# Output projection in three and five blocks, FF1 units between its tiles, an earlier x reload and a chained second product

## The chip, the cores and the metric

The kernel runs on one core of a Trainium2 chip. The metric is device time in microseconds (us); lower is better. Five engines work side by side, each through its own list in order: TensorE (PE, matrix products), VectorE (DVE), ScalarE (ACT), GpSimd (POOL) and SyncE (SP), whose list here is that of nearly all DMA transfers. PE takes its operands from SBUF and writes to banks of PSUM, which DVE or ACT then read.

## The reference

One layer over x of 1024 tokens x 1024 channels in float32:

```
u = rms_norm(x) @ W_in                    # columns split over three mixers
mixed = concat(stick_breaking_attention, retention, conformer_conv)
x = x + mixed @ W_out                     # 1024 x 1024
h = rms_norm(x)
x = x + square(relu(h @ W1)) @ W2         # 1024 x 4096 (FF1), 4096 x 1024 (FF2)
```

## The kernel before

All tensors are held transposed: channels on the 128 partitions, tokens along the free axis. Each float32 operand is split into a high part (cast to fp32r on ACT) and a low part (a subtraction on DVE or POOL), and each product is three matmuls, hi x hi, hi x lo, lo x hi (`mm3`, L107 to L110), mostly of 128x128 by 128x512. `w_split` (L141) splits weights, `x_split` (L703 to L706) splits quarters of x.

**Order of the work.** The program is written as a sequence, and a scheduler that simulates the engines reorders it for each engine (L1087). Buffers are named tiles (`xh0`, `P6`, `DM`, ...) of which one user must be through before the next writes; banks are named g, t, z, o, with two of each.

**Output projection** (L743 to L769). The mixed channels are eight blocks k of 128: attention 0 and 1, retention 2, 3, 6, 7, conv 4 and 5. Two passes of four blocks each. A pass has 16 tiles (8 of output channels, dt, times 2 halves of tokens, hf), each of 12 matmuls into a bank g and an addition to x2 (L758, the eviction). `tick` (L228) puts a tile among steps of attention, conv and retention that are still due. After each dt of the second pass `x2_ready` (L711) stores the tile to DRAM (x2d), squares it (ACT), adds the squares up (POOL, L720), scales it in place (ACT, L721) and forms the sums and differences that FF1 needs (POOL, L726 to L735; x_split). `x2_late` splits the rest.

**FF1.** Seven products of blocks (Strassen's scheme) instead of eight: 16 pairs p of 128-row tiles of W1, for each the products 1, 5, 6, 2, 7, 4, 3, each a unit of 12 matmuls over kk = 0 to 3, which read `x_split` tiles (i, kk). `hidden` makes the relu and its square, `right` forms the seven right operands of FF2 (POOL) and stores them as f{p}_{i} in DRAM.

**FF2.** Units are (chunk of pairs, product i, pair n), each with 12 matmuls into four banks. Five chunks of fifteen pairs go through the seven products in the order 5, 6, 3, 7, 1, 4, 2; products 1, 6 and 7 are gathered in separate accumulator tiles and added to the quadrants of x2 at the end by POOL (L964, L967). The last pair is done by eight plain block products (`run_last`, 96 matmuls). x is loaded back from DRAM when the first unit of FF2 is due (L1047 to L1055), `ahead` loads W2 tiles and f.

A `DMA` row of SP issues when its target is free and its source is ready; the rows behind it wait.

## Time and profile before

| | us |
|---|---|
| time, median of 3 runs | 1193.98 (1193.6 to 1194.81) |
| profiled execution, its own time | 1193.62 |
| its span | 1191.8 |
| PE busy | 1142.1 (96%) |
| DVE busy | 888.1 (75%) |
| POOL busy | 594.9 (50%) |
| ACT busy | 491.9 (41%) |

The span is what the profiler saw between the first and the last instruction; the rest of the execution's time lies around it. The mean granted clock of PE over the span is 0.984 of full speed (2.4 GHz); where the clock shows less, part of that stretch ran at 1.2 GHz. A share of busy time is a mean over stages. The output projection ends near 535, FF1 begins near 518 and ends near 862, FF2 ends at 1188.

### The profile page before, as it was taken

What the parts mean: (1) busy time and instruction counts of PE and PEld (TensorE: products, weight loads), DVE (VectorE), ACT (ScalarE), POOL (GpSimd) and SP (SyncE); (2) the same over time, 40 slices, a digit from 0 to 9 for tenths busy, and PEclk for the clock granted to TensorE, in tenths of its full rate; (3) what the DMA queues carried; (4) which work ended last, traced back from release to release, by engine and by line L of the source; (5) the groups of instructions that cost most, each with busy time, mean ns of one, the idle gap of its engine ahead of it and who ended that gap; (6) DMA issues with size and microseconds to landing.
All of it is one profiled execution on the core that took longest, in us unless ns stands there. A gap on an engine that the chain in (4) does not pass through costs nothing.

```text
span 1191.8 us, 17699 instructions
## 1 busy us (share of the span) xinstructions
PE 1142.1 (96%) x6388; PEld 991.6 (83%) x6388; DVE 888.1 (75%) x1346; ACT 491.9 (41%) x925; POOL 594.9 (50%) x473
## 2 busy tenths in 40 slices
...
GB/s 279 37 37 36 54 40 59 19 70 51 50 54 63 28 196 52 62 89 54 140 152 150 145 147 165 153 166 136 382 233 125 176 115 166 171 120 120 97 18 141
DMA packets 62871, 135.55 MB, mean 114 GB/s; under 512 B 7104, under 2 KB 11840, under 8 KB 62784
## 3 DMA queue, kind: packets, MB, share of 16 engines
...
q14 instruction: 37, 0.30, 0.1%
...
## 4 chain that ended last, share of the span: by engine, by line
PE 78%; DVE 13%; DMA 3%; issue 3%; ACT 2%; POOL 1%; SPq 0%; DVEq 0%; ACTq 0%; POOLq 0%
PE g L108 12%; PE g L110 12%; PE g L109 12%; PE t L108 4%; PE t L109 4%; PE t L110 4%; PE z L109 4%; PE z L110 4%; PE z L108 4%; PE o L109 3%; PE o L110 3%; PE o L108 3%; DVE DM__508_2651 L513 3%; DVE wlo L141 2%; PE o L354 2%
## 5 line engine op out<-in xcount | busy, mean ns | idle before, releaser
L141 POOL TENSOR_TENSOR wlo<-wraw,whi 128x512 fp32r<-128x512 f32 x67 | 100.3, 1510 | 96.4 <-ACT whi L140 96.2
L141 DVE TENSOR_TENSOR wlo<-sum,whi 128x512 fp32r<-128x512 f32 x75 | 77.3, 1032 | 86.9 <-ACT whi L140 86.9
L141 DVE TENSOR_TENSOR wlo<-wr,whi 128x512 fp32r<-128x512 f32 x88 | 86.9, 991 | 20.6 <-ACT whi L140 20.6
L140 ACT CAST whi<-sum 128x512 fp32r<-128x512 f32 x75 | 46.2, 618 | 115.5 <-POOL sum L783 48.1
L140 ACT CAST whi<-wr 128x512 fp32r<-128x512 f32 x88 | 53.3, 620 | 78.8 <-PE g L109 25.6
L324 POOL TENSOR_TENSOR be<-be,kp 128x512 f32<-128x512 f32 (+3 forms) x48 | 46.1, 962 | 78.3 <-DVE kp L320 49.9
L788 POOL TENSOR_TENSOR sum<-wr 128x512 f32<-128x512 f32 x16 | 22.7, 1419 | 98.8 <-DMA wr<-in_w_ff_dram 90.6
L140 ACT CAST whi<-wraw 128x512 fp32r<-128x512 f32 x68 | 41.9, 621 | 65.8 <-PE g L109 27.7
L320 DVE TENSOR_TENSOR_SCAN kp<-kp 128x512 f32<-128x512 f32 (+3 forms) x48 | 51.1, 1067 | 10.6 <-ACT kp L313 10.0
L513 DVE SCALAR_TENSOR_TENSOR DM__508_2651<-glu,vec,DM__508_2651 128x512 f32<-128x512 f32 x60 | 53.3, 926 | 0.1
L783 POOL TENSOR_TENSOR sum<-sum,wr 128x512 f32<-128x512 f32 x21 | 29.6, 1408 | 45.3 <-DVE wlo L141 45.3
L155 POOL TENSOR_TENSOR rs<-ss,nhalf 128x4 f32<-128x4 f32 (+1 forms) x36 | 37.9, 1055 | 25.4 <-DVE ss L621 14.5
L513 DVE SCALAR_TENSOR_TENSOR glu<-glu,vec 128x512 f32<-128x512 f32 x60 | 47.8, 857 | 0.0
L783 POOL TENSOR_TENSOR sum<-wr,sum 128x512 f32<-128x512 f32 x21 | 35.4, 1686 | 11.2 <-DVE wlo L141 11.2
L313 ACT ACTIVATE kp<-z 128x512 f32<-128x512 f32 (+3 forms) x48 | 23.6, 494 | 16.7 <-PE z L310 13.0
L108 PE MATMUL g<-whi,xh__12_100 128*128 128x256 f32 x82 | 25.3, 309 | 2.8 <-DVE P__107_556 L288 0.9
L108 PE MATMUL g<-whi,xh__34_250 128*128 128x256 f32 x82 | 23.3, 285 | 2.5 <-ACT xh__34_250 L174 2.5
L314 ACT ACTIVATE be<-z 128x512 f32<-128x512 f32 (+3 forms) x48 | 23.5, 493 | 4.9 <-PE t L335 4.9
L110 PE MATMUL g<-whi,xl__53_362 128*128 128x256 f32 x82 | 23.3, 286 | 1.6 <-DVE xl__53_362 L175 1.6
L335 PE MATMUL t<-ident,be 128*128 128x128 f32 x144 | 24.2, 274 | 0.1
L110 PE MATMUL g<-whi,xl__46_323 128*128 128x256 f32 x82 | 23.5, 288 | 0.0
L108 PE MATMUL g<-whi,xh__52_361 128*128 128x256 f32 x82 | 23.5, 287 | 0.0
...
## 6 DMA issues: line engine op xcount, KB each, us to landing
...
wraw<-in_w_in_dram SPq DMA_DIRECT2D x52, 256.0 KB, 3.2
...
wraw<-in_w_out_dram SPq DMA_DIRECT2D x16, 256.0 KB, 2.6
...
P__29_215<-in_xT_dram SPq DMA_DIRECT2D x1, 512.0 KB, 3.5
...
```

The source lines that it names most:

```text
L108: TE.matmul(out, lh, rh, start=start, stop=False, skip_group_check=on)
L109: TE.matmul(out, lh, rl, start=False, stop=False, skip_group_check=on)
L110: TE.matmul(out, ll, rh, start=False, stop=stop, skip_group_check=on)
L140: S.copy(hi, raw)
L141: (lo_engine or GP).tensor_tensor(out=lo, in0=raw, in1=hi.bitcast(F32), op=ALU.subtract)
L155: GP.tensor_tensor(out=out, in0=in_, in1=nhalf[:, 0:in_.shape[1]], op=ALU.pow)
L320: V.tensor_tensor_scan(rev, rev, rev, kp[:, n:n + 1], op0=ALU.mult, op1=ALU.bypass)
L324: GP.tensor_tensor(out=be[:, 0:n], in0=be[:, 0:n], in1=kp[:, 1:n + 1], op=ALU.mult)
L335: TE.transpose(pt[:, j * P:j * P + P], be[:, j * P:j * P + P], ident)
L354: TE.matmul(po[:, oc], lw, rhs, start=st["first"], stop=(jg == 0 and j == order[-1] and w is wtl))
L513: V.scalar_tensor_tensor(out=acc, in0=src, scalar=vec[:, o:o + 1], in1=acc, op0=ALU.mult, op1=ALU.add)
L783: (eng or GP).tensor_tensor(out=o, in0=x, in1=y, op=ALU.subtract)
```

## The change

1. The first pass takes blocks 0 to 2 (bank g, 9 matmuls in a tile), the second 3 to 7 (bank o, 15 matmuls). Weights come by quarters of a host-packed 512-column source; their low part is made on POOL in the first pass and on DVE in the second. Blocks are split by halves, 3, 4 and 5 inside the first pass.
2. The first three units of FF1 stand behind tiles dt = 5, 6, 7 of the second pass. The statistics of the second norm follow at unit 5. The `hidden` of product 2 of pair 0 moves to product 7, behind them.
3. In `x2_ready` the addition of squares (7 of 128x1024) and the first subtraction of dt >= 4 (4 of 128x512) go from POOL to DVE; two splits go to `x2_late`.
4. x is loaded back five units before the end of FF1, into other buffers. W2 and f loads follow written points (`transfers`), f with ten buffers instead of nine.
5. FF2 has four chunks (3, 4, 4, 5 pairs), all sixteen pairs by seven products, in the order 1, 5, 6, 3, 7, 2, 4. Products 1, 6, 7, 4 go on in one set of banks, 5 and 3 in the other, 2 after them; each intermediate sum is added to one quadrant of x2. The accumulator tiles, the POOL additions and `run_last` go.

The diff, cut to its core:

```diff
+    def w_quarter(lo_engine=None):
+
+        if not quarters:
+            c = wpos[1]
+            wpos[1] += 1
+            w_dma(c + RAW)
+            hi, lo = w_split(raws[c], lo_engine)
+            quarters.extend((hi[:, P * h:P * h + P], lo[:, P * h:P * h + P]) for h in range(4))
+        return quarters.pop(0)
...
+    def split_mixed(k, halves_=(0, 1)):
+        if k not in mh:
+            mh[k], ml[k] = slot(where[k][0], dt=F32R), slot(where[k][1], dt=F32R)
+        for hf in halves_:
+            cs = slice(512 * hf, 512 * hf + 512)
+            src = conv_part(k - 4, hf) if k in (4, 5) else mixed[k][:, cs]
+            S.copy(mh[k][:, cs], src)
+            V.tensor_tensor(out=ml[k][:, cs], in0=src, in1=mh[k][:, cs].bitcast(F32), op=ALU.subtract)
...
-    for k in range(4):
-        split_mixed(k)
-
-
-
-    XS = {1: ("xh0", "xl0", "xh1", "xl1"), 5: ("xh2", "xl2", "xh3", "xl3"), 6: ("P10", "P11", "P12", "P13"),
-          2: ("P14", "P15", "P16", "P17"), 7: ("P18", "P19", "P4", "P5"), 4: ("P0", "P1", "P2", "P3"),
-          3: ("P6", "P7", "P8", "P9")}
+    split_mixed(0)
+    for hf in range(2):
+        for k in (1, 2):
+            split_mixed(k, (hf,))
...
-            sq2[0] = pg.tile([P, T], F32, tag="glu0", name="sq2")
-            S.activation(sq2[0], x, AF.Square)
+            sq = sq2[0] = pg.tile([P, T], F32, tag="glu0", name="sq2")
         else:
             sq = slot(("DM", "glu1")[dt % 2])
-            S.activation(sq, x, AF.Square)
-            GP.tensor_tensor(out=sq2[0], in0=sq2[0], in1=sq, op=ALU.add)
+        S.activation(sq, x, AF.Square)
...
-            return
-        t, b12 = x2[kk][:, 0:512], x2[kk][:, 512:1024]
-        GP.tensor_tensor(out=t, in0=b, in1=t, op=ALU.subtract)
-        x_split(6, kk, t)
-        x_split(2, kk, a)
-        GP.tensor_tensor(out=b12, in0=b, in1=b12, op=ALU.subtract)
-        x_split(7, kk, b12)
-        GP.tensor_tensor(out=t, in0=a, in1=t, op=ALU.subtract)
+        else:
+            t, b12 = x2[kk][:, 0:512], x2[kk][:, 512:1024]
+            V.tensor_tensor(out=t, in0=b, in1=t, op=ALU.subtract)
+            x_split(6, kk, t)
+            x_split(2, kk, a)
+            GP.tensor_tensor(out=b12, in0=b, in1=b12, op=ALU.subtract)
+            if kk < 2:
+                x_split(7, kk, b12)
+            GP.tensor_tensor(out=t, in0=a, in1=t, op=ALU.subtract)
+        if dt > 0:
+            V.tensor_tensor(out=sq2[0], in0=sq2[0], in1=sq, op=ALU.add)
...
     def x2_late():
+        for kk in range(2, 4):
+            x_split(7, kk, x2[kk][:, 512:1024])
         for kk in range(4):
             x_split(4, kk, x2[kk][:, 0:512])
         for kk in range(4):
             x_split(3, kk, x2[kk + 4][:, 512:1024])
 
...
-    pend = parts(4)
-    for pi in range(2):
-        for dt in range(NK):
-            w = pend[:2]
-            del pend[:2]
-            for hf in range(2):
-                tsl = slice(512 * hf, 512 * hf + 512)
-
-                def run():
-                    ps = bank("g")
-                    for q in range(4):
-                        k = 4 * pi + q
-                        cs = slice((q % 2) * P, (q % 2) * P + P)
-                        wh, wl = w[q // 2]
-                        mm3(ps, wh[:, cs], wl[:, cs], mh[k][:, tsl], ml[k][:, tsl], q == 0, q == 3)
-                    V.tensor_tensor(out=x2[dt][:, tsl], in0=ps, in1=x2[dt][:, tsl], op=ALU.add)
-                    if wpos[1] < len(sources) or halves:
-                        pend.append(w_part())
-                tick(run)
-            if pi == 1:
-                x2_ready(dt)
-        if pi == 0:
-            while steps:
-                tick()
-            for k in range(4, 8):
-                split_mixed(k)
-    x2_late()
...
+
+    def out_weights(pi, dt):
+        ks = range(EARLY) if pi == 0 else range(EARLY, NK)
+        return {k: w_quarter(GP if pi == 0 else V) for k in ks}
+
+    def out_proj(pi, dt, hf):
+        tsl = slice(512 * hf, 512 * hf + 512)
+        w = taken[pi, dt]
+        ps = bank("o" if pi else "g")
+        for k in w:
+            mm3(ps, w[k][0], w[k][1], mh[k][:, tsl], ml[k][:, tsl], k == min(w), k == max(w))
+        V.tensor_tensor(out=x2[dt][:, tsl], in0=ps, in1=x2[dt][:, tsl], op=ALU.add)
+
+    jobs = [(pi, dt) for pi in range(2) for dt in range(NK)]
+    taken[0, 0] = out_weights(0, 0)
+
+    def out_job(pi, dt):
+        n = jobs.index((pi, dt))
+        if n + 1 < len(jobs):
+            taken[jobs[n + 1]] = out_weights(*jobs[n + 1])
+        for hf in range(2):
+            tick(lambda: out_proj(pi, dt, hf))
+        if pi == 1:
+            x2_ready(dt)
+
+    for dt in range(NK):
+        out_job(0, dt)
+        if dt in (1, 5, 6):
+            split_mixed({1: 3, 5: 4, 6: 5}[dt])
+    while steps:
+        tick()
+    for hf in range(2):
+        for k in (6, 7):
+            split_mixed(k, (hf,))
...
-    chunks = [[0, 1], [2, 3, 4], [5, 6, 7, 8], [9, 10, 11], [12, 13, 14]]
-    order2 = (5, 6, 3, 7, 1, 4, 2)
+
+    chunks = [[0, 1, 2], [3, 4, 5, 6], [7, 8, 9, 10], [11, 12, 13, 14, 15]]
+    order2 = (1, 5, 6, 3, 7, 2, 4)
...
-    WS2 = [("wr", 4)] * 4 + [(t, 1) for t in XS[4] + XS[3]]
-    nw2 = [0]
-    nfi = [0]
-    FI = ("DM", "xh4", "xl4", "xh5", "xl5", "xh6", "xl6", "xh7", "xl7")
+    C = XS[1] + XS[5]
+    WS2 = (["wr", "wr"] + list(XS[7] + XS[4] + XS[3]) + ["wr", "wr", "DM", "P4", "P5"])
+    WS2 = ["wr", "wr", "glu0", "DM", "P4", "P5"] + WS2 * 2
+    RS = XS[6][2:4] + XS[2][0:2]
+    FI = FS[0] + XS[2][2:4] + FS[1]
+    nw2, nfi, nrs, nsum = [0], [0], [0], [0]
 
...
     def run_ff2(c, i, n):
-        s = {5: "X", 3: "X", 1: "X", 2: "X", 6: "Y", 7: "Y", 4: "Y"}[i]
-        first = i in (5, 1, 6, 4)
+        s = {1: "X", 6: "X", 7: "X", 4: "X", 5: "Y", 3: "Y", 2: "Y"}[i]
+        first = i in (1, 5, 2)
         if n == 0 and first:
             ps2[s] = [bank(t) for t in {"X": "ggtt", "Y": "zzoo"}[s]]
...
+        rh, ch = {1: (0, 0), 2: (0, 0), 5: (1, 1), 7: (1, 1), 6: (0, 1), 3: (0, 1), 4: (1, 0)}[i]
         for dt in range(4):
-            ps = ps2[s][dt]
-            if i in (1, 6, 7):
-                a = a_part(i, dt)
-                if c == 0:
-                    S.copy(a, ps)
-                else:
-                    add(a, a, ps)
-            else:
-                a = c_part({5: 5, 3: 3, 2: 2, 4: 4}[i], dt)
-                add(a, ps, a)
-        if c == len(chunks) - 1 and i == 1:
-            for dt in range(4):
-                for to, src in ((6, 1), (7, 1)):
-                    GP.tensor_tensor(out=a_part(to, dt), in0=a_part(to, dt), in1=a_part(src, dt), op=ALU.add)
-            for to, src in ((3, 6), (4, 7), (5, 7)):
-                for dt in range(4):
-                    GP.tensor_tensor(out=c_part(to, dt), in0=c_part(to, dt), in1=a_part(src, dt), op=ALU.add)
-
...
-    def run_last(k, dh):
-        for dt in range(4):
-            ps = bank(("z", "o", "g", "t")[dt])
-            cs = slice(dt * P, dt * P + P)
-            for j in range(2):
-                wh, wl = last_w[dh][j]
-                fh, fl = last_f[k][j]
-                mm3(ps, wh[:, cs], wl[:, cs], fh, fl, j == 0, j == 1)
-            a = c_part({(0, 0): 2, (0, 1): 4, (1, 0): 3, (1, 1): 5}[k, dh], dt)
-            add(a, ps, a)
-            r = (4 * dh + dt) * P
-            nc.sync.dma_start(d["yT"][r:r + P, 512 * k:512 * k + 512], a)
+            a = x2[4 * rh + dt][:, 512 * ch:512 * ch + 512]
+            add(a, ps2[s][dt], a)
+            if c == len(chunks) - 1 and i in (3, 7, 2, 4):
+                r = (4 * rh + dt) * P
+                nc.sync.dma_start(d["yT"][r:r + P, 512 * ch:512 * ch + 512], a)
...
+    prep = {"1": prep_ff1, "2": prep_ff2}
+    run = {"1": run_ff1, "2": run_ff2}
+    f_order = [(chunks[c][n], i) for c in range(len(chunks)) for i in order2 for n in range(len(chunks[c]))]
+    nf = [0]
...
+    w2_at = {n1 + 6: 3, n1 + 10: 4, n1 + 14: 5, n1 + 18: 6, n1 + 25: 7, n1 + 29: 8, n1 + 33: 9, n1 + 37: 10,
+             n1 + 41: 11, n1 + 53: 12, n1 + 57: 13, n1 + 61: 14, n1 + 65: 15}
+
+    def f_upto(n):
+        while nf[0] < min(n, len(f_order)):
+            load_f(*f_order[nf[0]])
+            nf[0] += 1
+
+    def transfers(n):
+
+        v = units[n + 2] if n + 2 < len(units) else None
+        if v and v[0] == "1" and v[2] == 6 and v[1] + 2 < npair:
+            load_w1(v[1] + 2)
+        if n == n1 - 7:
+            load_w2(0)
+            load_w2(1)
+            f_upto(3)
+        if n == n1 - 5:
+            for dt in range(NK):
+                x2[dt] = slot(C[dt])
+                nc.sync.dma_start(x2[dt], x2d[dt])
+        if n == n1 - 4:
+            load_w2(2)
+            f_upto(4)
+        if n == n1 - 2:
+            f_upto(6)
+        if n >= n1:
+            f_upto(n - n1 + 2 + len(FI))
+        if n in w2_at:
+            load_w2(w2_at[n])
 
...
+    def mlp(n):
+        transfers(n)
+        if n + 2 < len(units):
+            prep[units[n + 2][0]](*units[n + 2][1:])
+        run[units[n][0]](*units[n][1:])
+
+    for dt in range(NK):
+        if dt == 5:
+            for u in units[:2]:
+                prep[u[0]](*u[1:])
+        out_job(1, dt)
+        if dt >= 5:
+            mlp(dt - 5)
+    x2_late()
+    for n in range(3, len(units)):
+        if n == 5:
             row_stats(sq2[0], mse2, rstd2, bank("o"))
             rbc2 = pg.tile([P, T], F32, tag="glu1", name="rbc2")
...
-        run[u[0]](*u[1:])
+            row_bcast(rbc2, rstd2, "o", "kp")
+        mlp(n)
```

How the rows of the engines' lists move. DVE, at the end of the output projection, before: `xl7__833` is the last tile of x2, `g_1024` and `g_1025` its two banks, `P..` the x_split tiles (L706), `wlo` low parts of FF1's weights (L141).

```order
L758 TENSOR_TENSOR xl7__833_5231<-g_1024_6154,xl7__833_5231 128x512
L141 TENSOR_TENSOR wlo_1078_6354<-wr_1039_6226,whi_1077_6353 128x512
L706 TENSOR_TENSOR P19__1017_6105<-xl4__827_5213,P19__1017_6105 128x512
L706 TENSOR_TENSOR P16__1022_6146<-xh7__832_5228,P16__1022_6146 128x512
L706 TENSOR_TENSOR P0__1030_6199<-xh4__826_5210,P0__1030_6199 128x512
L706 TENSOR_TENSOR P7__1035_6214<-xl6__831_5225,P7__1035_6214 128x512
L758 TENSOR_TENSOR xl7__833_5231<-g_1025_6168,xl7__833_5231 128x512
L706 TENSOR_TENSOR P6__1034_6211<-xh6__830_5222,P6__1034_6211 128x512
L141 TENSOR_TENSOR wlo_1082_6373<-wr_1039_6226,whi_1081_6372 128x512
```

Five rows stand between the two evictions. The same place after: `o_1044` and `o_1045` are the last two tiles' banks (eviction L774), L743 the subtraction and L751 the addition of squares that ran on POOL, L721 the splits. `P11` is the split for product 2, kk = 3.

```order
L774 TENSOR_TENSOR xl7__833_5231<-o_1044_6219,xl7__833_5231 128x512
L153 TENSOR_TENSOR wlo_1073_6344<-wr_966_5783,whi_1072_6343 128x512
L743 TENSOR_TENSOR xh5__828_5216<-xh7__832_5228,xh5__828_5216 128x512
L721 TENSOR_TENSOR P10__1040_6195<-xh7__832_5228,P10__1040_6195 128x512
L721 TENSOR_TENSOR P6__1039_6192<-xh5__828_5216,P6__1039_6192 128x512
L153 TENSOR_TENSOR wlo_1082_6385<-wr_966_5783,whi_1081_6384 128x512
L721 TENSOR_TENSOR xh3__1059_6295<-xh5__828_5216,xh3__1059_6295 128x512
...
L774 TENSOR_TENSOR xl7__833_5231<-o_1045_6236,xl7__833_5231 128x512
L721 TENSOR_TENSOR P16__1067_6319<-xh7__832_5228,P16__1067_6319 128x512
...
L751 TENSOR_TENSOR sq2_5831<-sq2_5831,glu1__1046_6254 128x1024
L743 TENSOR_TENSOR xl5__829_5219<-xl7__833_5231,xl5__829_5219 128x512
L721 TENSOR_TENSOR P11__1048_6261<-xl7__833_5231,P11__1048_6261 128x512
```

Between the last two evictions there are eight rows now; behind the last one an addition of squares and a subtraction stand ahead of `P11`.

PE at the same place, before: the end of the last tile `g_1025`, then FF1's first unit `g_1050` in the other bank g, and the next one, `g_1063`, which takes the bank of `g_1025`.

```order
L110 MATMUL g_1025_6168<-P8__969_5824,wlo_1012_6075 128x512
L108 MATMUL g_1050_6248<-xh0__976_5866,whi_1043_6234 128x512
L109 MATMUL g_1050_6248<-xh0__976_5866,whi_1043_6234 128x512
...
L110 MATMUL g_1050_6248<-xl1__1000_6004,wlo_1044_6235 128x512
L108 MATMUL g_1063_6294<-xh0__976_5866,whi_1048_6244 128x512
L109 MATMUL g_1063_6294<-xh0__976_5866,whi_1048_6244 128x512
```

So the eviction of `g_1025` is needed one unit after its end. After: the last matmul of the last tile `o_1045`, then units of FF1 (z_1071, t_1074, g_1028, t_1095), and the first that reads `P11`.

```order
L110 MATMUL o_1045_6236<-P2__963_5772,wlo_1035_6150 128x512
L109 MATMUL z_1071_6329<-P14__991_5941,whi_1041_6202 128x512
...
L110 MATMUL z_1071_6329<-P15__1002_5999,wlo_1042_6203 128x512
L108 MATMUL t_1074_6347<-P4__1009_6048,whi_1051_6272 128x512
...
L108 MATMUL g_1028_6130<-P8__1010_6051,whi_1069_6325 128x512
...
L108 MATMUL t_1095_6491<-P4__1009_6048,whi_1088_6429 128x512
...
L110 MATMUL t_1095_6491<-P6__1039_6192,wlo_1089_6430 128x512
L108 MATMUL g_1028_6130<-P11__1048_6261,whi_1069_6325 128x512
```

The next unit to take a bank no longer needs that of the last tile; 32 matmuls stand between `o_1045` and `P11`.

SP at the change from FF1 to FF2, before: L1052 loads x2d back, L891 W2, L899 f; L810 stores f.

```order
L899 DMA xh7__1510_8901<-f1_7_6588 128x512
L1052 DMA xh0__1518_8919<-x2d0_5212 128x1024
L891 DMA wr_1492_8826<-in_w_ff2_dram 128x1024
L899 DMA xl7__1511_8903<-f0_1_6456 128x512
L1052 DMA xl0__1519_8920<-x2d1_5215 128x1024
...
L899 DMA DM__1512_8905<-f1_1_6575 128x512
...
L899 DMA xh4__1495_8832<-f1_5_6582 128x512
L891 DMA P1__1514_8909<-in_w_ff2_dram 128x1024
...
L899 DMA xl4__1496_8834<-f0_6_6466 128x512
```

W2 and f loads are mixed with the x loads. After: L1004 loads x2d, L921 W2, L929 f; L837 stores f. Rows of 128x1024 are 512 KB, of 128x512 256 KB. Between f1_1 and f15_3 stand nine rows of L921.

```order
L837 DMA f13_4_8571<-xl7__1425_8436 128x512
L1004 DMA xh1__1488_8788<-x2d0_5212 128x1024
L1004 DMA xl1__1489_8790<-x2d1_5215 128x1024
L921 DMA wr_1558_9099<-in_w_ff2_dram 128x1024
...
L929 DMA xh4__1474_8741<-f0_1_6468 128x512
...
L929 DMA xl4__1475_8743<-f1_1_6587 128x512
L921 DMA P13__1577_9197<-in_w_ff2_dram 128x1024
...
L921 DMA P17__1695_9757<-in_w_ff2_dram 128x1024
L837 DMA f15_3_8921<-xl6__1482_8768 128x512
L837 DMA f15_2_8923<-xl6__1482_8768 128x512
L837 DMA f15_5_8926<-xh7__1483_8769 128x512
L929 DMA xh5__1476_8745<-f2_1_6751 128x512
```

Both begin the reload directly behind the store of `f13_4`; after it the x loads follow each other with fewer rows between, and f1_1 is followed by nine W2 loads and three stores (f15_3, f15_2, f15_5) before `xh5__1476`, the load of f2_1.

## Rows read from the trace of the kernel before

**Rows 1.** the page's first part, busy time by engine
```profile
PE 1142.1 (96%) x6388; PEld 991.6 (83%) x6388; DVE 888.1 (75%) x1346; ACT 491.9 (41%) x925; POOL 594.9 (50%) x473
```

**Rows 2.** windows: length, busy (count) of PE, PEld, DVE, ACT, POOL; clock, DMA, GB/s
```profile
480.00:492.00 12.00, 9.25 (x36) 7.28 (x35) 4.27 (x6) 2.37 (x4) 4.74 (x5) 0.86 0.01 1
518.00:570.00 52.00, 41.00 (x162) 30.97 (x161) 46.70 (x42) 27.72 (x43) 39.80 (x22) 0.90 0.20 71
570.00:848.00 278.00, 278.00 (x1228) 230.21 (x1227) 179.13 (x237) 100.95 (x175) 160.91 (x116) 1.00 0.48 161
848.00:886.00 38.00, 23.58 (x72) 16.58 (x71) 23.76 (x25) 11.07 (x20) 21.27 (x15) 0.73 0.80 302
886.00:1155.00 269.00, 268.15 (x1183) 221.71 (x1182) 228.65 (x314) 118.39 (x210) 79.38 (x51) 1.00 0.43 131
1155.00:1188.00 33.00, 30.62 (x127) 24.52 (x125) 23.78 (x29) 1.14 (x2) 19.63 (x14) 0.95 0.30 112
834.00:874.00 40.00, 29.01 (x112) 21.89 (x111) 29.00 (x34) 12.47 (x22) 26.82 (x19) 0.88 0.94 361
```

**Rows 3.** waits of PE, 480 to 570: total us, times, longest us
```profile
PE g L108 <- DVE xl__833_5231 L758: 6.4, 2, 5.4
...
PE o L109 <- DVE P__1032_6205 L706: 2.4, 1, 2.4
```

**Rows 4.** timeline, 481 to 485: start, duration (us), engine, line, operation
```profile
481.51 0.60 PE L543 MATMUL t<-ident,cv 128*128 128x128 f32 x4
...
483.43 0.73 POOL L551 TENSOR_TENSOR DM__508_2651<-e,e 128x256 f32<-128x256 f32 x1
...
484.19 0.62 ACT L682 CAST P__963_5808<-DM__508_2651 128x512 fp32r<-128x512 f32 x1 [0.18 <-POOL DM__508_2651 L551]
...
484.86 0.50 PE L108 MATMUL g<-P__963_5808,whi 128*128 128x512 f32 x1 [2.75 <-ACT P__963_5808 L682]
```

**Rows 5.** timeline, end of the output projection
```profile
534.49 0.39 PE L110 MATMUL g<-P__969_5824,wlo 128*128 128x512 f32 x1
534.65 2.84 POOL L720 TENSOR_TENSOR sq<-sq,DM__1020_6138 128x1024 f32<-128x1024 f32 x1
...
540.83 1.71 POOL L733 TENSOR_TENSOR xh__828_5216<-xh__832_5228,xh__828_5216 128x512 f32<-128x512 f32 x1
...
541.33 1.74 DVE L706 TENSOR_TENSOR P__1030_6199<-xh__826_5210,P__1030_6199 128x512 fp32r<-128x512 f32 x1
543.00 0.68 DVE L706 TENSOR_TENSOR P__1035_6214<-xl__831_5225,P__1035_6214 128x512 fp32r<-128x512 f32 x1
543.60 0.68 DVE L758 TENSOR_TENSOR xl__833_5231<-g,xl__833_5231 128x512 f32<-128x512 f32 x1
...
544.34 0.79 PE L108 MATMUL g<-xh__976_5866,whi 128*128 128x512 f32 x1 [5.41 <-DVE xl__833_5231 L758]
```

**Rows 6.** timeline of ACT, the first x tile
```profile
495.70 1.15 ACT L721 ACTIVATE xh__826_5210<-xh__826_5210,vec 128x1024 f32<-128x1024 f32 x1 [0.30 <-DMA x2d<-xh__826_5210]
```

**Rows 7.** waits of PE, 848 to 890
```profile
PE z L109 <- DVE P__1517_8916 L909: 4.9, 1, 4.9
PE t L108 <- DVE kp L817: 3.5, 1, 3.5
```

**Rows 8.** timeline of SP, first x load and f load
```profile
834.67 0.40 SPq L1052 DMA_DIRECT2D xh__1518_8919<-x2d  x1
...
852.05 0.32 SPq L899 DMA_DIRECT2D xh__1495_8832<-f  x1
```

**Rows 9.** DMA 820 to 890, 40 slices; one issue: KB, us to landing
```profile
GB/s 204 228 167 0 0 167 282 150 186 401 274 403 414 389 265 378 425 403 406 414 409 416 419 407 419 411 406 420 397 183 11 36 208 55 0 124 380 317 227 215
...
xh__1495_8832<-f SPq DMA_DIRECT2D x1, 256.0 KB, 7.0
```

**Rows 10.** timeline, the last matmul, add and store
```profile
1187.53 0.39 PE L110 MATMUL t<-P__2067_11500,wlo 128*128 128x512 f32 x1
...
1188.03 0.69 DVE L817 TENSOR_TENSOR xl__1525_8926<-t,xl__1525_8926 128x512 f32<-128x512 f32 x1 [0.51 <-PE t L110]
1188.75 0.33 SPq L989 DMA_DIRECT2D out_dram<-xl__1525_8926  x1
```

More of the change, by code (lines that the diff above doesn't have):

```diff
@@ L114, in build @@
     sources = [d["w_in"][g, :, 512 * c:512 * c + 512] for g in range(len(GROUPS)) for c in range(4)]
-    sources += [d["w_out"][dt, :, 512 * p:512 * p + 512] for p in range(2) for dt in range(NK)]
+    sources += [d["w_out"][i] for i in range(2 * NK)]
     raws = {}
@@ L838, in run_ff1 @@
         elif i == 7:
+            if p == 0:
+                hidden(u1[p, "f"][0][:, 0, :], ps1[p, "g"], 0)
             u1[p, 3] = small("kp", (P, 512), 2)
@@ L844, in run_ff1 @@
         elif i == 2:
-            hidden(u1[p, "f"][0][:, 0, :], ps, 0)
+            if p > 0:
+                hidden(u1[p, "f"][0][:, 0, :], ps, 0)
         elif i == 4:
```

96 lines of the change are left out of this document (14 added, 82 removed).

## The prediction

> **What bounds the kernel now.** I read the table of engines first: TensorE (PE) is busy 1142.1 of 1191.8 us [rows 1]. So only two things shorten the span: fewer matmuls, or fewer holes on PE. The table of windows gives both. In the untroubled stretch 570 to 848 there are 1228 matmuls in 278.00 us, which is 0.2264 us for each with 512 columns [rows 2]. In any other window the time minus count x 0.2264 is what PE lost there (a matmul with fewer columns is counted too dearly, so a loss is a little larger than stated):
> - 480:492, end of the first pass of the output projection: 12 - 36 x 0.2264 = 3.9
> - 518:570, second pass and beginning of the first product (FF1): 52 - 162 x 0.2264 = 15.3
> - 848:886, from FF1 to the second product (FF2): 38 - 72 x 0.2264 = 21.7
> - 886:1155, middle of FF2: 269 - 1183 x 0.2264 = 1.2
> - 1155:1188, its end: 33 - 127 x 0.2264 = 4.2
>
> Together 46.3 us. Part is half clock: the granted clock is 0.90 in 518:570 and 0.73 in 848:886 [rows 2], that is, PE ran at 1.2 GHz for a while after each hole. A hole that goes takes its half clock with it.
>
> Then I asked who ends the waits. In the second window it is VectorE (DVE): 5.4 us for an eviction of the last out-projection tile and 2.4 us for an x_split [rows 3]. In the third it is again DVE by name (kp 3.5 us, the split P__1517 4.9 us) [rows 7], but the split waits for a load. From 834 to 874 the DMA engines are 0.94 busy at 361 GB/s [rows 2].
>
> **A. Fewer matmuls.** FF2 had 15 pairs x 7 products x 12 and 96 plain ones, 1356. Now it is 16 x 84 = 1344. 12 x 0.2264 = **-2.7 us**. The out projection keeps its count (16 x 9 + 16 x 15 = 384 = 32 x 12).
>
> **B. First pass.** PE waited 2.75 us at 484.86 for the cast of the last conv part. The chain is PE's last transposes 481.51, POOL's product 483.43, ACT's cast 484.19 [rows 4]. With three blocks in the first pass and five in the second, that cast is still the last to come, but two tiles can run their block 3 ahead of it. On the other side, pass 1 is 16 x 3 matmuls shorter and so has less work to lie beside the conv chain. Bounds: 0.5 (hole gone) to 8 (twice as long). I take 3.5, near the row: **-0.4**.
>
> **C. Second pass and start of FF1.** Before, the last eviction (L758) began at 543.60 though its matmuls had ended at 534.9 (534.49 + 0.39): it stood in DVE's queue behind x_splits, and PE resumed at 544.34 [rows 5]. The change puts the tiles of pass 2 in another bank ("o") than the FF1 unit that follows, so PE does not wait for this eviction any more. It goes on with FF1 units. What is late next is the x_split of the last x tile: in the new order 32 matmuls (z_1071's rest to t_1095) stand between the end E of the last tile o_1045 and the first that reads P11, which is 7.2 us of cover. P11 is the second of the two splits that end the stretch of DVE shown there. After the eviction of o_1044 (at E - 15 x 0.2264 = E - 3.4) DVE has 8 instructions, then the eviction of o_1045, then 8 more of 512 columns and one addition of squares of 1024, which the change took from POOL.
>
> What does one cost? A subtraction with both inputs in SBUF took 0.68 us alone (543.00) and 1.74 us beside a POOL subtraction of 1.71 us (541.33 and 540.83); the eviction, with one input in PSUM, stayed at 0.68 [rows 5]. The addition of squares has no DVE row; POOL's took 2.84 [rows 5]. I bound it by twice a 512 one: 1.36 to 3.48.
> - All at 0.68: E - 3.4 + 0.7 + 5.4 = E + 2.7, eviction to E + 3.4, then 5.4 + 1.4 gives E + 10.2, a hole of 2.9 us.
> - All at 1.74: E + 11.2, E + 11.9, then 13.9 + 3.5 gives E + 29.3, a hole of 22 us.
> - I take 0.9, nearer to alone, since the change empties POOL of the seven additions of squares and four subtractions that ran beside DVE. That gives E + 14.2, a hole of 7 us.
>
> The way through the DMA and ACT (ACT's scaling waits for the copy of the tile to DRAM, and is 1.15 us [rows 6]) is shorter than that queue. With 2 us for half clock and statistics C loses 9 instead of 15.3: **-6.3**, with ends -11 and +8.7.
>
> On this the Trainium skill, *SBUF — State Buffer*, section "Who interferes with whom", says that a VectorE instruction with two SBUF inputs contends with a GpSimd instruction that reads SBUF, and that the second to start fully blocks. Our pair agrees (0.68 became 1.74 beside 1.71), and the rule speaks against moving work to DVE: by it, each of the moved operations pays whenever POOL is busy. It bears on the second rival.
>
> **D. From FF1 to FF2.** Call T the end of FF1 on PE. Before, the reload of x was first issued at 834.67, some 18 us ahead of where FF1's matmuls would have ended; a load of f of 256 KB issued at 852.05 landed 7.0 us later [rows 8, 9]. Every SP transfer goes through one queue in order, and the queue is full. The change starts the reload five units earlier in the program, but SP works in order, and in both orders the first x load stands directly behind the store of f13_4: it can move little, and with less mixed in among the x loads I put it at T - 20. Then I count what stands in SP's order from there up to f2_1, which the third unit of FF2 needs: 24 transfers of 512 KB and 15 of 256 KB, 16.5 MB. At the 400 to 420 GB/s that the full slices show [rows 9], 16.5 MB take 40 us; at the window's 361 GB/s, 46. So f2_1 lands at T + 20 to T + 26, and I take T + 22, since nine loads of w2 and three stores of f15 stand directly ahead of it. f0_1 and f1_1 are before those: by the same count 8.7 and 10.7 MB, T + 2 to T + 8. So PE has two units (5.4 us) to do, and starts the third at about T + 23: 17.6 lost, about 3 at half clock, 1.2 for the next f load: 22 in place of 21.7, **+0.3**. Ends: 5 (rival 1) and 47 (rival 3).
>
> The Trainium skill, same page, section "Summary: rules for kernel authors", advises to reckon HBM transfers at about 358 GB/s. The full slices here show more, 400 to 420 [rows 9], and they decide; by the page's figure the 16.5 MB would take an estimated 46 us.
>
> **E, F. Middle and end of FF2.** Chaining 1, 6, 7, 4 and 5, 3 in PSUM takes out the accumulator tiles, with their copies, and all 20 POOL additions at the end. Boundaries of chunks go from 4 to 3: 1.2 becomes 1.0, **-0.2**; bounds 0 and 5, if a bank is read late at each boundary. At the end stood those additions and four plain block products; now five pairs run in a row for each product, with evictions of 0.69 us [rows 10] beside other units: 4.2 becomes 0.2, **-4.0**, bounds 0 and 4.2. The tail is unchanged: last matmul 1187.53, add 1188.03, store 1188.75, end 1191.8 [rows 10].
>
> **Sum.** -2.7 - 0.4 - 6.3 + 0.3 - 0.2 - 4.0 = -13.3. Against the profiled execution's own 1193.62 us (span 1191.8 and 1.8 around it) that is 1180.3. The median of the runs shown, 1193.98, lies 0.4 higher: **1180.7 us**.
>
> **Rivals.**
> 1. The start of FF2 clears. If the loads of f overtake (the w2 loads' targets free early, or f2_1 needs less than the queue ahead of it), D loses 5, not 22: 1180.7 - 17 = **1164**. For it: two f loads stand ahead of the w2 block, and the x loads need no wait on PE at the end. Against it: the 0.94 share in the window, and that nothing in the order lets f2_1 pass nine w2 loads.
> 2. VectorE becomes the bound of pass 2. At a mean of 1.3 us for the 8 + 8 instructions and 2.6 for the addition, P11 comes at E + 21.4, a hole of 14 and 16 lost: C is +0.9 and the time **1188**. For it: DVE was busy for 46.7 of the 52 us already [rows 2]. Against it: POOL, the other half of each pair, is relieved.
> 3. Slower: SP stands still ahead of the f loads. Four w2 loads go to pages that hold x for the last FF1 unit and are free only at T; SP waits for them in order, and stores of f15 that wait for POOL follow. If the engines are then idle so that the 16.5 MB run at 245 GB/s instead of 410, f2_1 lands at T + 47: D is +25, time **1206**. It decides from 16.5 MB in 54 us, 305 GB/s, where the -13.3 are used up. Against it: in the same stretch before, with ten w2 loads in the same queue, the window still moved 361 GB/s [rows 2].
> 4. The change does not do what it says: the earlier reload is pushed back by SP's order. That is in the forecast, which gives it 3 us only.
>
> **How the numbers follow.** Forecast 0.52 (its own range 1173 to 1188), rival 1 0.14, rival 2 0.22, rival 3 0.06; 0.06 is left for small mixtures on either side. Two tenths of a per cent, 2.4 us, is what this kernel's runs can tell from no change. Faster takes the forecast, rival 1 and most of rival 2: 0.88. Same 0.04: rival 2 with a mean near 1.6 us. Slower 0.08: rival 3 and rival 2 at its bound. Range: rival 1 begins at 1164 and the upper part of rival 2 at 1190; I go from 1166 to 1190.
>
> **What would show it.** A: 1344 matmuls of FF2. C: after the last out-projection tile PE goes straight on with FF1 units and its next wait is for P11 by DVE, 3 to 12 us. D: granted clock below 1 and one long wait, about 15 us, on the split of f2_1 after exactly two units of FF2, with DMA share over 0.9 before it. F: no PE hole over 1 us in the last 33 us. I am wrong if PE waits for "o" banks inside pass 2, if the long wait is missing or sits at another f, or if it is over 30 us.

## The result and the profile after

The changed kernel takes 1180.58 us (median; 1179.3 to 1183.48), the kernel before 1194.39 beside it (1193.6 to 1196.64). The ratio is 0.9885 (95% interval 0.9862 to 0.9908): 1.15% faster. The profiled execution took 1179.3 us, its span 1177.4.

The page's first part after, to be read against [rows 1]: 12 matmuls fewer, and DVE a little less busy in spite of what it took over.

```profile
PE 1131.6 (96%) x6376; PEld 984.6 (84%) x6376; DVE 867.1 (74%) x1347; ACT 489.8 (42%) x925; POOL 541.9 (46%) x440
```

The windows after, shifted with the program, against [rows 2] (length, busy (count) of PE, PEld, DVE, ACT, POOL; clock, DMA share, GB/s):

```profile
465.00:485.00 20.00, 19.78 (x88) 15.44 (x87) 13.55 (x26) 8.31 (x14) 5.54 (x7) 1.00 0.19 53
510.00:570.00 60.00, 53.33 (x228) 42.42 (x228) 51.66 (x64) 32.09 (x52) 28.40 (x17) 0.94 0.29 100
570.00:835.00 265.00, 263.74 (x1164) 218.12 (x1163) 168.79 (x222) 96.31 (x167) 155.29 (x112) 1.00 0.48 158
835.00:880.00 45.00, 25.97 (x94) 19.40 (x93) 23.43 (x28) 11.52 (x20) 26.56 (x18) 0.81 1.00 387
880.00:1150.00 270.00, 269.76 (x1187) 222.13 (x1186) 220.83 (x299) 112.47 (x198) 79.96 (x50) 1.00 0.41 125
1150.00:1174.00 24.00, 23.59 (x105) 19.20 (x103) 10.85 (x18) 4.74 (x9) 0.00 (x0) 1.00 0.16 58
825.00:872.00 47.00, 26.71 (x102) 19.87 (x101) 27.27 (x32) 12.23 (x22) 27.48 (x19) 0.85 1.00 387
```

By the same rule (time less count x 0.2264) PE now loses: 0.1 at the end of the first pass (3.9 before); 8.4 in the second pass and the beginning of FF1 (15.3); 1.5 + 23.7 = 25.2 from FF1 to FF2 (21.7); 1.3 in the middle of FF2 (1.2); 0.2 at its end (4.2). With the 12 matmuls, -2.7, that is -2.7 - 3.8 - 6.9 + 3.5 + 0.1 - 4.0 = -13.8 of the 14.3 us between the two profiled executions.

PE's waits at the out projection (430 to 600), against [rows 3] (total, times, longest):

```profile
PE t L110 <- DVE wlo L153: 5.4, 1, 5.4
PE t L108 <- ACT whi L152: 1.1, 1, 1.1
```

and from FF1 to FF2, against [rows 7]:

```profile
PE g L108 <- ACT P__1512_8878 L935: 8.8, 1, 8.8
PE g L108 <- ACT P__1525_8953 L935: 6.2, 1, 6.2
PE z L108 <- DVE xl__1482_8768 L844: 1.6, 1, 1.6
PE g L108 <- ACT P__1516_8901 L935: 1.6, 1, 1.6
```

P__1512 and P__1525 are the splits of f0_1 and f2_1. The SP rows for the reload and those two loads, against [rows 8], and how long they took to land, against [rows 9]:

```profile
825.78 0.38 SPq L1004 DMA_DIRECT2D xh__1488_8788<-x2d  x1
...
843.64 0.32 SPq L929 DMA_DIRECT2D xh__1474_8741<-f  x1
...
862.51 0.32 SPq L929 DMA_DIRECT2D xh__1476_8745<-f  x1
```

```profile
xh__1474_8741<-f SPq DMA_DIRECT2D x1, 256.0 KB, 7.4
...
xh__1476_8745<-f SPq DMA_DIRECT2D x1, 256.0 KB, 7.6
```

FF1's last matmul, whose end is T:

```profile
844.99 0.39 PE L110 MATMUL z<-P__1068_6322,wlo 128*128 128x512 f32 x1
```

The reload begins at 825.78, 19.6 us ahead of T (844.99 + 0.39 = 845.4). f2_1 lands at 862.51 + 7.6 = 870.1 = T + 24.7. The DMA share from 825 to 872 is 1.00, at 387 GB/s. The end, against [rows 10]: the last matmul, add and store keep their distances.

```profile
1173.21 0.39 PE L110 MATMUL t<-P__2042_11524,wlo 128*128 128x512 f32 x1
1173.63 0.69 DVE L844 TENSOR_TENSOR P__1495_8802<-t,P__1495_8802 128x512 f32<-128x512 f32 x1
...
1174.35 0.33 SPq L972 DMA_DIRECT2D out_dram<-P__1495_8802  x1
```

### The profile page after: what moved, and what is told of

Its sections match the earlier page's. It is cut to its first block, busy times and chain, and to the rows that moved or that the text cites. A ratio compares the mean times of both kernels' runs of the same rounds, so it can differ in the third digit from the quotient of the medians.

```text
span 1177.4 us, 17628 instructions
## 1 busy us (share of the span) xinstructions
PE 1131.6 (96%) x6376; PEld 984.6 (84%) x6376; DVE 867.1 (74%) x1347; ACT 489.8 (42%) x925; POOL 541.9 (46%) x440
## 4 chain that ended last, share of the span: by engine, by line
PE 73%; DVE 12%; DMA 6%; issue 4%; POOL 2%; ACT 2%; SPq 0%; DVEq 0%; ACTq 0%; POOLq 0%
PE g L108 12%; PE g L110 11%; PE g L109 11%; PE t L108 4%; PE t L110 4%; PE t L109 4%; PE z L109 3%; PE z L110 3%; PE z L108 3%; PE o L108 3%; PE o L109 3%; PE o L110 3%; DVE wlo L153 3%; PE o L366 2%; PE t L347 1%
## 5 line engine op out<-in xcount | busy, mean ns | idle before, releaser
L153 DVE TENSOR_TENSOR wlo<-sum,whi 128x512 fp32r<-128x512 f32 x78 | 78.9, 1011 | 95.0 <-ACT whi L152 91.2
L153 POOL TENSOR_TENSOR wlo<-wraw,whi 128x512 fp32r<-128x512 f32 x57 | 86.2, 1527 | 78.0 <-ACT whi L152 75.5
L153 DVE TENSOR_TENSOR wlo<-wr,whi 128x512 fp32r<-128x512 f32 x80 | 79.0, 993 | 12.1 <-ACT whi L152 12.1
L152 ACT CAST whi<-wr 128x512 fp32r<-128x512 f32 x80 | 48.2, 619 | 56.0 <-PE g L109 16.8
L167 POOL TENSOR_TENSOR rs<-ss,nhalf 128x4 f32<-128x4 f32 (+1 forms) x36 | 37.3, 1038 | 30.2 <-DVE ss L633 15.3
L810 POOL TENSOR_TENSOR sum<-wr,sum 128x512 f32<-128x512 f32 x19 | 32.0, 1684 | 7.5 <-DVE wlo L153 7.5
L108 PE MATMUL g<-whi,xh__12_100 128*128 128x256 f32 x82 | 25.3, 309 | 2.8 <-DVE P__107_556 L300 0.9
L810 POOL TENSOR_TENSOR sum<-sum,wr 128x512 f32<-128x512 f32 x18 | 25.2, 1402 | 3.0 <-DVE wlo L153 3.0
L108 PE MATMUL g<-whi,xh__34_250 128*128 128x256 f32 x82 | 23.4, 285 | 1.7 <-ACT xh__34_250 L186 1.7
L110 PE MATMUL g<-whi,xl__53_362 128*128 128x256 f32 x82 | 23.3, 286 | 1.6 <-DVE xl__53_362 L187 1.6
L110 PE MATMUL g<-whi,xl__46_323 128*128 128x256 f32 x82 | 23.4, 287 | 0.4 <-DVE xl__46_323 L187 0.4
L109 PE MATMUL g<-wlo,xh__52_361 128*128 128x256 f32 x82 | 23.5, 287 | 0.0
```

The source lines that it names most:

```text
L108: TE.matmul(out, lh, rh, start=start, stop=False, skip_group_check=on)
L109: TE.matmul(out, lh, rl, start=False, stop=False, skip_group_check=on)
L110: TE.matmul(out, ll, rh, start=False, stop=stop, skip_group_check=on)
L152: S.copy(hi, raw)
L153: (lo_engine or GP).tensor_tensor(out=lo, in0=raw, in1=hi.bitcast(F32), op=ALU.subtract)
L167: GP.tensor_tensor(out=out, in0=in_, in1=nhalf[:, 0:in_.shape[1]], op=ALU.pow)
```

## The experiments

All times are medians of four or more executions. Ratios are to the kernel before, which ran beside each group; the changed kernel has 0.9885 (0.9862 to 0.9908).

**e1, additions of squares and first subtractions back on POOL.**

```diff
-            V.tensor_tensor(out=t, in0=b, in1=t, op=ALU.subtract)
+            GP.tensor_tensor(out=t, in0=b, in1=t, op=ALU.subtract)
-            V.tensor_tensor(out=sq2[0], in0=sq2[0], in1=sq, op=ALU.add)
+            GP.tensor_tensor(out=sq2[0], in0=sq2[0], in1=sq, op=ALU.add)
```

> The changed kernel with the seven additions of squares and the four subtractions of dt >= 4 back on POOL. Theory M (the gain at the out projection comes from FF1 units lying between its tiles and from the other bank; the moved additions cost DVE 1.2 us each and are paid for by less contention): within 3 us of the changed kernel's 1180.6, the wait after the last tile between 3 and 8 us, DVE instructions beside POOL at 1.74 more often. Rival V (VectorE is the bound there and the move to it costs time): 4 to 8 us faster, about 1175, the wait after the last tile gone.

1184.88 us (1184.34 to 1188.21), ratio 0.9927 (0.9901 to 0.9953): some 4 us slower than the changed kernel, with intervals of the ratios that overlap a little. V falls, and M's "within 3" is missed as well. The five additions between 500 and 556 took 7.20 us on DVE and take 12.41 on POOL; the four subtractions took 3.84 and take 6.49. DVE is hardly relieved: it is busy for 45.55 us there instead of 47.92, though 11.0 us of work have left it. Its weight splits (L153) in that stretch, first in the changed kernel, then in e1 (length, busy (count) of DVE and ACT, clock, DMA share, GB/s):

```profile
500.00:556.00 56.00, 9.61 (x12) 0.00 (x0) 0.94 0.25 86
```

```profile
500.00:556.00 56.00, 14.43 (x11) 0.00 (x0) 0.94 0.21 76
```

That is 0.80 us each against 1.31; the x_splits go from 22 in 22.69 to 20 in 26.82. So the two kinds of split take 9 us more, with three fewer of them done, for the 11.0 that left. The longest wait of PE there is 7.6 us in place of 5.4, and the two weight splits at its end show why: the first, beside an addition of squares on POOL, takes 2.82 us, the second 0.68, 3.42 together. In the changed kernel both took 0.68 (at 544.79 and 546.00).

```profile
545.25 2.78 POOL L751 TENSOR_TENSOR sq<-sq,glu__1046_6254 128x1024 f32<-128x1024 f32 x1
...
545.76 3.42 DVE L153 TENSOR_TENSOR wlo<-sum,whi 128x512 fp32r<-128x512 f32 x2
```

**e2, second pass in bank g.**

```diff
-        ps = bank("o" if pi else "g")
+        ps = bank("g")
```

> The changed kernel with the second pass's tiles in bank g again. Theory M says that the bank is a part of the gain: FF1 units that use g then wait for an eviction that stands in DVE's queue, 4 to 8 us slower, about 1186. Rival W (what gained is only that units lie between the tiles; with cover the eviction is done in time in any bank): within 2 us of 1180.6.

1186.9 us (1185.2 to 1187.46), ratio 0.9938 (0.9915 to 0.9961): M holds, in size too. The waits of PE from 430 to 600 show where:

```profile
PE o L216 <- DVE sq L751: 4.4, 1, 4.4
PE g L108 <- DVE xl__833_5231 L774: 1.7, 1, 1.7
PE g L108 <- ACT xh__947_5700 L696: 1.4, 1, 1.4
...
PE g L109 <- DVE xl__948_5701 L697: 0.5, 1, 0.5
```

The eviction of the last tile (xl__833) is waited for again, as in [rows 3], and so is the cast of the last conv part (xh__947), the hole of [rows 4]. The longest wait, 4.4 us, is that of the norm's statistics for the last addition of squares. From 465 to 485 PE loses 3.2 us (74 matmuls) where the changed kernel loses 0.1, and from 500 to 585 it loses 10.5 (329 matmuls) against 8.0. The traces show how the bank bears on the first of these. Below are the first matmul of the second pass and the last cast of block 4 (the conv part) in the changed kernel, then that first matmul in e2:

```profile
454.22 0.48 PE L108 MATMUL o<-xh__909_5529,whi 128*128 128x512 f32 x1
...
475.37 0.62 ACT L696 CAST xh__947_5700<-DM__508_2651 128x512 fp32r<-128x512 f32 x1 [0.18 <-POOL DM__508_2651 L563]
```

```profile
468.36 0.48 PE L108 MATMUL g<-xh__909_5529,whi 128*128 128x512 f32 x1
```

So term B's hole comes back without the other bank. Whether the bank alone would close it in the kernel before was not run.

**e3, units behind the tiles.**

```diff
         out_job(1, dt)
-        if dt >= 5:
-            mlp(dt - 5)
     x2_late()
-    for n in range(3, len(units)):
+    for n in range(len(units)):
```

> The changed kernel with the first three FF1 units behind the last tile of the out projection, bank o kept. Theory M: the cover of 32 matmuls behind the last tile is smaller or the scheduler moves the units in between by itself; written order alone decides 3 to 8 us: 1184 to 1188. Rival S (the scheduler orders by readiness, so where the program writes the units makes no difference): within 2 us of 1180.6.

1179.69 us (1179.06 to 1184.55), ratio 0.9888 (0.9859 to 0.9918): S holds. The place in the program made no difference; the same 5.4 us wait stands at the same matmul.

**e4, the splits for products 4 and 3 held behind P11.**

```diff
         t = slot(XS[i][kk], (P, 2, 512), F32R)
+        if i in (4, 3):
+            S.copy(t[:, 0, 0:1], xr[2, 3][:, 1, 0:1].bitcast(F32))
```

> The changed kernel with the eight x_splits for products 4 and 3 held behind the split P11 (a copy of one column makes them depend on it), so they no longer stand in DVE's queue ahead of the weight splits that PE needs next. Theory Q (the 5.4 us wait behind the last tile is DVE's queue of work that is not urgent): that wait falls to 0 to 2 us and the time by 3 to 6 us, to about 1176. Rival L (DVE's total work sets it; the held splits are then late for products 4 and 3 of pair 0): a wait of like size moves to those units, within 2 us of 1180.6.

1181.43 us (1181.01 to 1182.72), ratio 0.9896 (0.9874 to 0.9918): L's time holds, its reason does not: nothing waits for products 4 and 3. The wait for the weight split is gone, but PE then waits for the broadcast of the norm's statistics, whose operand DVE makes (L224):

```profile
PE o L226 <- DVE kp L224: 3.6, 1, 3.6
PE t L108 <- ACT whi L152: 1.9, 1, 1.9
```

The queue that theory Q named is real, but behind it the chain of the last tile to the statistics is almost as late.

**e11, four and four blocks.**

```diff
-        for k in (1, 2):
+        for k in (1, 2, 3):
...
-    EARLY = 3
+    EARLY = 4
...
-        if dt in (1, 5, 6):
-            split_mixed({1: 3, 5: 4, 6: 5}[dt])
+        if dt in (5, 6):
+            split_mixed({5: 4, 6: 5}[dt])
...
-    parts = [w_out[k, :, dt] for ks in (range(3), range(3, NK)) for dt in range(NK) for k in ks]
+    parts = [w_out[k, :, dt] for ks in (range(4), range(4, NK)) for dt in range(NK) for k in ks]
```

> The changed kernel with four and four blocks in the two passes of the output projection, all else kept. Term B of the prediction put the split of three and five at 0.4 us: 1180 to 1183, with a wait of 2 to 4 us for the conv part's cast at the end of the first pass. Rival: the three-block pass is what lets tiles fill the conv chain and pass 2's longer tiles cover DVE; four and four costs 4 to 8 us, about 1186.

1181.13 us (1178.8 to 1182.5), ratio 0.9894 (0.9878 to 0.991): no difference, and no wait for the conv cast either (430 to 500 shows none). Its rival falls, and the wait that the expectation named did not come. Three and five is not what closed that hole.

**e8, only FF2 changed on the kernel before**: with `run_ff2` of the changed kernel, without `run_last` and the accumulators.

```diff
-    chunks = [[0, 1], [2, 3, 4], [5, 6, 7, 8], [9, 10, 11], [12, 13, 14]]
-    order2 = (5, 6, 3, 7, 1, 4, 2)
+    chunks = [[0, 1, 2], [3, 4, 5, 6], [7, 8, 9, 10], [11, 12, 13, 14, 15]]
+    order2 = (1, 5, 6, 3, 7, 2, 4)
...
-    WS2 = [("wr", 4)] * 4 + [(t, 1) for t in XS[4] + XS[3]]
+    WS2 = [("wr", 4)] * 4 + [(t, 1) for t in XS[4] + XS[3] + XS[6] + XS[2][2:4]]
```

> The kernel before with only the second product changed: four chunks of all sixteen pairs, the chained order, no accumulator tiles, the freed pages as further W2 buffers. Terms A and F of the prediction say 2.7 + 4.0 us less in the last 33 us and in the matmul count, so about 1187.5, if the start of FF2 stays as it was. Rival: the freed pages let still more W2 loads ahead of f (SP's order has fourteen there), and the start of FF2 loses 5 to 15 us: 1192 to 1203 with the end as clean as forecast.

1185.77 us (1183.28 to 1187.13), ratio 0.994 (0.9921 to 0.996), -0.6%, some 7 us: A and F alone, 6.7. By the windows the loss from 890 on is 0.6 us, all of it at the end, and the start of FF2 loses 22.6 (52 - 130 x 0.2264), near the 21.7 of before; its rival falls.

```profile
838.00:890.00 52.00, 34.56 (x130) 26.04 (x129) 33.38 (x40) 17.42 (x30) 33.39 (x23) 0.80 0.97 373
890.00:1155.00 265.00, 265.00 (x1171) 219.43 (x1170) 218.89 (x296) 110.80 (x195) 76.12 (x48) 1.00 0.44 130
1155.00:1181.00 26.00, 25.17 (x112) 20.50 (x110) 10.92 (x18) 4.57 (x8) 0.00 (x0) 1.00 0.21 76
```

**e5, e6, e7: the order of the loads.** e5 rotates the f buffers, e6 holds W2 loads, e7 does both.

```diff
-    FI = FS[0] + XS[2][2:4] + FS[1]
+    FI = XS[2][2:4] + FS[0] + FS[1]          # e5, e7
...
+            if 3 <= p <= 8:                  # e6, e7
+                S.copy(t[:, 0:1], x2[0][:, 0:1])
             nc.sync.dma_start(t, d["w_ff2"][2 * p + j])
```

> The changed kernel with the list of buffers for f rotated: the first two loads take P10 and P11, so f2_1 takes the first page that frees and stands ahead of the nine W2 loads in SP's queue. Theory Q (the long waits at the start of FF2 are set by the order in SP's queue, f2_1 behind nine W2 loads): f2_1 lands some 19 us earlier, the first four units run before the block, the next wait is for f1_5 behind it, and 4 to 8 us go: 1173 to 1177. Rival B (the bytes to be moved bound the stage, so that any order costs the same): within 2 us of 1180.6, the wait only changes its name.

> The changed kernel with the loads of W2 for pairs 3 to 8 (twelve of 512 KB) held until the first eviction of FF2 (a copy of one column of x2 into the page makes the load wait for it). Theory Q: f2_1 stands behind 6.3 MB less, lands some 10 to 15 us earlier, and the time falls by 8 to 12 us, to 1169 to 1173; nothing waits for the late W2 loads, which the second chunk needs some 50 us later. Rival B: the bytes come back as waits of the second and third product, within 3 us of 1180.6.

> Both of the two edits on loads together. Theory Q: f0_1, f1_1 and f2_1 all land near the end of FF1, what is left is the wait for the first (ACT's and DVE's queue and the landing, 3 to 6 us) and half clock: 12 to 17 us faster than the changed kernel, 1164 to 1169. Rival B: no better than the better one of the two.

1178.84 (1177.64 to 1180.04), 1180.66 (1179.67 to 1182.13) and 1179.29 (1173.53 to 1179.85); ratios 0.989 (0.9855 to 0.9924), 0.9903 (0.9873 to 0.9932) and 0.9879 (0.9843 to 0.9916). All three miss the times that theory Q expected and look like rival B. The windows tell more. From 820 to 950 the changed kernel loses 25.4 us (130 - 462 x 0.2264), e5 22.7 (474 matmuls), e6 19.3 (489) and e7 19.7 (487). e5's longest wait there is for f1_5 (4.9 us), as theory Q said, but it gains only 2.7. e6 gains 6 us there; its profiled execution, at 1179.67, gives 2 back between 950 and 1150 and 4 at the out projection, where its instructions are those of the changed kernel (last section). f2_1 landed at 857.0 in e6, and PE does not wait for it any more. It waits for

```profile
PE g L108 <- ACT P__1556_9078 L937: 6.4, 1, 6.4
PE z L108 <- DVE xl__1482_8768 L844: 5.6, 1, 5.6
```

P__1556 is the split of f1_6, which the eighth unit needs, and xl__1482 an eviction of FF1's last pair. SP's rows show why: the W2 loads of three pairs, let go by one eviction, stand ahead of it (xl__1518) with only two stores of f among them, and its load took 8.2 us to land.

```profile
868.76 0.33 SPq L923 DMA_DIRECT2D wr<-in_w_ff_dram  x1
...
869.65 0.38 SPq L923 DMA_DIRECT2D wr<-in_w_ff_dram  x1
870.13 0.43 SPq L923 DMA_DIRECT2D P__1576_9197<-in_w_ff_dram  x1
870.65 0.80 SPq L923 DMA_DIRECT2D P__1577_9200<-in_w_ff_dram  x1
871.55 0.44 SPq L923 DMA_DIRECT2D xh__1594_9294<-in_w_ff_dram  x1
872.08 0.40 SPq L923 DMA_DIRECT2D xl__1595_9297<-in_w_ff_dram  x1
...
873.01 0.42 SPq L931 DMA_DIRECT2D xl__1518_8939<-f  x1
```

So the block only moved. Whether it or the sum of bytes is the bound, these three do not tell apart. One of e7's four executions took 1173.53, near what its window gained; it has no trace, so its cause is open.

**e9, e10, e12: the W2 loads one pair after the other.** Each pair from 3 to 8 waits for the eviction of the product before it in the program. e9 has e5's rotation as well, e10 gives f0_1 and f1_1 pages that are free ahead of the x reload, e12 has the stagger alone:

```diff
+    recent = [None]
...
+            if 3 <= p <= 8:
+                S.copy(t[:, 0:1], recent[0][:, 0:1])
             nc.sync.dma_start(t, d["w_ff2"][2 * p + j])
...
             add(a, ps2[s][dt], a)
+            recent[0] = a
...
-    C = XS[1] + XS[5]                        # e10 only, and the next two
+    C = XS[1][2:4] + XS[5] + XS[2][2:4]
-    FI = FS[0] + XS[2][2:4] + FS[1]
+    FI = XS[1][0:2] + FS[0] + FS[1]
```

> The rotated f buffers of e5, and the W2 loads of pairs 3 to 8 held one pair after the other, each until the product before it in the program has been evicted, in place of all twelve at one time. Theory Q2 (a block of W2 loads in the queue starves f wherever it stands; in e6 and e7 it only came later): no second long wait, the start of FF2 loses 10 to 14 us in place of 20 to 25, the time 1168 to 1173. Rival B (the sum of bytes bounds the stage; f, stores and W2 together need what the queue gives): within 3 us of e7's 1179, with several small waits.

> As e9, and f0_1 and f1_1 go to pages that free at the end of product 1 of the last pair, ahead of the x reload in SP's queue; two x tiles take pages that free later. Theory Q2: the first wait of FF2 is no longer for f0_1, the start of FF2 loses 5 to 9 us, the time 1163 to 1170. Rival B: the x reload and the first W2 loads are late in their turn, within 2 us of e9.

> The staggered W2 loads of e9 without its rotated f buffers. Theory Q2 (the block of W2 loads is the cause, the buffers only decide which f stands behind it): f2_1 still waits for its page to free and for the stores ahead of it, some 3 to 6 us at the second or third unit, and the time is 1170 to 1175. Rival: the rotation is needed for most of e9's gain, 1177 to 1181.

1169.24 (1168.01 to 1171.57), 1168.27 (1166.32 to 1169.79) and 1168.46 (1165.38 to 1169.96); ratios 0.9797 (0.9778 to 0.9815), 0.9787 (0.9772 to 0.9802) and 0.9789 (0.9764 to 0.9813). B falls: the same bytes cost 11 to 12 us less than in the changed kernel once no block of W2 loads stands ahead of f. e12 shows that the stagger alone does it, a little better than was expected for it: the wait for f2_1 that was expected does not come. e10's pages added nothing: from 820 to 950 it loses 12.5 us (519 matmuls), e9 11.6 (523) and e12 11.4, where 5 to 9 were expected of e10. All three beat both kernels. From 820 to 950, first the changed kernel, then e12, both with FF1 at the same place:

```profile
820.00:950.00 130.00, 109.71 (x462) 88.41 (x461) 93.72 (x121) 47.10 (x83) 61.26 (x41) 0.93 0.67 237
```

```profile
820.00:950.00 130.00, 121.21 (x524) 99.12 (x523) 108.64 (x132) 52.88 (x103) 72.08 (x48) 0.97 0.72 245
```

62 matmuls more in the same 130 us, at 245 GB/s against 237. What PE waits for longest from 820 to 950 in e12 is no load any more but DVE's evictions in FF1's last pairs:

```profile
PE z L108 <- DVE xl__1482_8768 L844: 6.0, 1, 6.0
PE z L108 <- DVE xl__1449_8594 L844: 1.4, 1, 1.4
PE g L108 <- ACT P__1640_9498 L939: 1.4, 1, 1.4
```

## Why the prediction was right, and where it was not

The forecast of -13.3 us came out as -13.8 by the same windows. Two of its six terms were mis-sized in opposite directions, B by -3.4 and D by +3.2; that they cancel is luck, and the total is better than the working. By its own signs the prediction was wrong at D: the one long wait of about 15 us after exactly two units did not come, and the longest wait sits at another f.

- **A**, -2.7: shown by the count, 6388 to 6376.
- **B**, -0.4 expected, -3.8 measured: the term was mis-sized, since its reason was the wrong one. The prediction ascribed what might be gained to the blocks of the passes. e11 shows that these make no difference, e2 that the bank does: with the tiles of the two passes in different banks, the second pass begins 21 us ahead of the conv part's last cast (454.22 and 475.37) and fills the time in which it is made.
- **C**, -6.3 expected, -6.9 measured. The mechanism is shown: no wait for the last eviction any more, and a wait of 5.4 us (3 to 12 expected) behind DVE's queue after it. It is not the wait for P11 that was forecast: PE stopped three rows ahead of P11 in DVE's list, at a weight split, and at P11 itself it did not wait again. P11's split ended at 551.19, 17.2 us behind the last tile's end (534.0), where 14.2 had been reckoned. DVE's x_splits took 1.03 us on average and its weight splits 0.80, near the 0.9 that was taken.

  The -6.9 has luck in it too: it is from an execution in which PE came back to full clock early, and in others the same stretch loses some 4 us more (last section), which would leave C at about -3. The prediction took 0.9 us since POOL was emptied; e1 shows what that is worth: without it a weight split takes 1.31 us, the mean of rival 2, and the kernel some 4 us more. The Trainium skill, *SBUF — State Buffer*, "Who interferes with whom", states the rule on pairs: a VectorE instruction with two SBUF inputs contends with a GpSimd instruction that reads SBUF. The traces agree: the first of the two weight splits ahead of PE's wait took 0.68 us with POOL idle and 2.82 in e1, beside the addition on POOL. Rival 2 did not come.
- **D**, +0.3 expected, +3.5 measured. Right: the reload's start (T - 20, measured T - 19.6), the full queue, and the range for f2_1's landing (T + 20 to 26, measured T + 24.7). Mis-sized: the point taken in that range, T + 22. The 16.5 MB took 44.3 us from the first issue to that landing, 372 GB/s, nearer the window's 361 than the full slices' 400 to 420. The third unit began at 870.81, T + 25.4 in place of T + 23, which is 2.4 of the 3.2 us. Wrong: that PE has its first two units to do at T + 2 to T + 8 and then waits once. f0_1 landed at 843.64 + 7.4 = 851.0 = T + 5.6, but ACT cast it only at 853.48: it stood in ACT's queue behind squares of the last pair, which waited for DVE. f1_1 landed at 849.75 + 6.3 = T + 10.7.

```profile
847.32 0.63 ACT L842 ACTIVATE xl__1482_8768<-xl__1482_8768 128x512 f32<-128x512 f32 x1 [1.98 <-DVE xl__1482_8768 L840]
...
850.66 0.63 ACT L842 ACTIVATE xl__1482_8768<-xl__1482_8768 128x512 f32<-128x512 f32 x1 [2.20 <-DVE xl__1482_8768 L840]
852.94 0.63 ACT L842 ACTIVATE xh__1481_8767<-xh__1481_8767 128x512 f32<-128x512 f32 x1 [1.65 <-DVE xh__1481_8767 L840]
853.48 0.60 ACT L935 CAST P__1512_8878<-xh__1474_8741 128x512 fp32r<-128x512 f32 x1
```

  So PE waited 8.8 us for the first unit and 6.2 for the third, in place of one long wait of 15. That split the wait but added little to it, since the third unit had to wait for f2_1 either way. The cause that was given, f2_1 behind nine W2 loads, was one step short. e6 shows that f2_1 ahead of them moves a wait on to the f behind them; e12 shows that the block itself is the cause. Rival 1's 1164 was not far off for a kernel without it (1168.5), but the change as made cannot get there, as was argued.
- **E** and **F**, -0.2 and -4.0 expected, +0.1 and -4.0 measured; e8 shows A and F by themselves.
- What was said of the program's order, that units between the tiles give cover, holds for the engine's list but not for the place in the source: e3.

Rival 3 (SP stands still) did not come: the share was 1.00. What is left open is why the stretch behind the 5.4 us wait differs between executions (last section); how much of e1's 4 us it is, and of e6's median, the runs do not tell.
